# A two-layer hybrid diffusion step on one Trainium2 core: grouped-query products before the expansions, a two-operation silu, state products first, prompt scores in the value bank

## The chip, the cores and the metric

The kernel runs on one core of one Trainium2 chip. The metric is the device time of one execution in microseconds, as the median of several runs. A profile is one execution taken by the hardware profiler; its busy times are of the core's engines: PE (matrix products), DVE (vector), ACT (scalar functions and copies), POOL, and SP, whose queue issues DMAs.

## What is computed

One inference step over 128 prompt tokens and 512 noisy latent tokens, two layers of width 1024. Each layer is a modulated RMSNorm, one input projection, two branches side by side, one output projection and a gated residual. Layer 0 has multi-head latent attention (8 heads) and grouped-query attention (8 heads on 2 key heads); layer 1 has a bidirectional mLSTM and differential attention. The parts of the reference that the change touches:

```
u = h @ w_in
cq, ckv, kr, g_a, q_b, k_b, v_b, g_b = split_cols(u, EVEN_SPLITS)
q = (rmsnorm(cq, qn_g) @ w_uq)                      # expansion of the queries
q_b = rmsnorm(q_b.reshape(B, S, GQA_HEADS, GQA_HD), gq_g)
kv = (ckv_all @ w_ukv)                              # expansion of keys and values
o_a = attend(q_a, k_a, v_a) * jax.nn.silu(g_a)
o_b = attend(q_bg, kb_all, vb_all) * jax.nn.silu(g_b)
x + gate * (concatenate([o_a, o_b]) @ w_out)
# mLSTM: num = w_inter * (C q) + (Sm v)
```

## The kernel before

All products are made in float32 with operands split into a high and a low part, so that each is three matrix products (`mm3`, L81; lines L83, L84, L85): high by high, high by low, low by high. The five token groups of 128 (group 0 is the prompt) stand side by side.

The kernel is written as a program of tiles. A planner orders each engine's queue when the kernel is built, by the order in which the program states the instructions and by its own estimate of when each is ready; every engine then works through its queue in that order. Two tools bind it: `pe_order` (L162) fixes PE's order to the program's in the attention of layer 0, and `issue_after` puts the instructions of a block that run on one engine behind a given instruction of that engine.

The stages of layer 0, in order. `even_linear` (L342): the norm and modulation, then piece A of the input projection (compressed queries), piece B (compressed keys and values, grouped keys and values; `evB` L504), the query expansion in two halves (`evQ` L543), the value expansion (L553, its six results copied by DVE, L559), the key expansion (L561, copied by ACT), and piece C (grouped queries; `evC` L575: copy, sum of squares, norm, rotary embedding). Each result waits in one of five PSUM accumulators until ACT or DVE has copied it. `even_prep` (L768) builds the key tiles of the attention. `even_gates` (L591) makes the gate products and applies silu to each (`silu_from` L123).

`attention` (L699) runs over 16 heads. The scores of a head's four query blocks (L621) go to a ring of two score tiles (`s2`); DVE takes the row maximum (L628), ACT the exponential (L631), DVE the reciprocal (L634), POOL the scaling (L641). PE then transposes the scaled blocks (L648, `head_T`) into a ring of two (`t1`), ACT or DVE copies them (L653, L651), and PE multiplies them by the values (L659, `head_PV`) into the single tile `o`. While it transposes head h, the loop issues scores of heads h+1 and h+2. `prep` makes the split keys (`keys` L782, whose low part is a POOL subtraction, L789) and queries of head h+2. Four prompt quads (L663) go through four stages each between the heads; their scores (L672) take one of the two `s2` tiles. `side` (L860) adds the modulation products of layer 1, the gate products of layer 0 (L234), and loads and splits of the output projection's weights (L893); after head 15 it makes the row of residual gates (`ada_gate_row` L238, sum at L248). Then `out_proj` (L897) starts, with its accumulators in the PSUM banks of the attention.

In layer 1, `odd_linear` (L1035) makes the differential keys (`o_wK`), queries (`o_wQ`), values (`o_wV1`) and the mLSTM values (`o_wVM`); the mLSTM's scans over its gates (`mlstm_gates` L1221, on DVE and PE) are stated after the first of these. `mlstm_head` (L1447) makes, for each of five token groups, the product of scores and values (L1508, tile `pv`) and of state and query (tile `it`), and DVE adds the two (L1520); between them `adv` issues products of later pieces as filling, behind the instruction in `self.mark`.

Of the kernel before, what the change touches and what calls it, by code (L numbers as in the profile page):

```python
# [37 lines left out]
class K:  # L38
# [84 lines left out]
    def silu_from(self, out, src, shape, pool, other=None):  # L123

        nc = self.nc
        th = pool.tile(shape, F32, tag="th", name="th", bufs=2)
        nc.scalar.activation(out=th, in_=src, func=AF.Tanh, scale=0.5)
        nc.vector.tensor_scalar(out=th, in0=th, scalar1=0.5, scalar2=0.5, op0=ALU.mult, op1=ALU.add)
        nc.vector.tensor_tensor(out=out, in0=th, in1=src, op=ALU.mult)
        if other is not None:  # L130
            nc.vector.tensor_tensor(out=out, in0=out, in1=other, op=ALU.mult)
# [106 lines left out]
    def ada_gate_row(self, L, pool, tag, bufs):  # L238
# [9 lines left out]
        nc.vector.tensor_tensor(out=row, in0=ps[:, 0:256], in1=bias, op=ALU.add)  # L248
        for g in range(4):
            nc.sync.dma_start(self.gd[L][:, g * 256:g * 256 + 256], row[32 * g:32 * g + 2])  # L250
# [91 lines left out]
    def even_linear(self, E, EM, H, L, ps):  # L342
# [198 lines left out]

        for hf in range(2):
# [11 lines left out]
        for t in range(6):  # L554
# [4 lines left out]
            nc.vector.tensor_copy(Va[:, t, :], acc)  # L559
# [12 lines left out]

        self.qb = E.tile([128, 5, 512], F32, tag="qb", name="qb", bufs=1)

        def evC(t, acc):  # L575
            q = self.qb[:, t]
            nc.scalar.copy(q, acc)
            qv = q.rearrange("p (h w) -> p h w", h=8)
            r = self.rsqrt(self.sumsq(q, 8, 64), 8, 64)
            nc.vector.tensor_tensor(out=qv, in0=qv, in1=r[:, :, None].to_broadcast([128, 8, 64]), op=ALU.mult)  # L580
            nc.vector.tensor_tensor(out=qv, in0=qv, in1=self.rows[:, None, R_GQ:R_GQ + 64].to_broadcast([128, 8, 64]),
                                    op=ALU.mult)
            if t:
                self.rope(qv, qv, *ropeB(t), 8, 64, L)

        self.lin_tok([(A["e_wC"][i], 2) for i in range(4)], 512, Hh, Hl, range(5), evC, ps)

# [49 lines left out]
    def head_scores(self, T, ps, passes, i):  # L637
# [3 lines left out]
        self.nc.gpsimd.tensor_tensor(out=p, in0=p, in1=rs.to_broadcast([128, 640]), op=ALU.mult)  # L641
# [21 lines left out]
    def prompt_quad(self, T, ps, prep, V, cols, m):  # L663
# [4 lines left out]
        s = ps.tile([128, 2, 512], F32, tag="s2", name="sp", bufs=2)[:, 0]  # L668
# [1016 lines left out]
```

## Time and profile before

| | us |
|---|---|
| median of 3 runs | 885.71 |
| lowest and highest run | 885.25, 886.45 |
| the profiled execution, its own time | 888.68 |
| its span, first to last instruction | 886.9 |
| PE busy in the span | 839.8 |

A row of the waits names who waited, and the instruction that came last before it could go on. A row of a timeline merges neighbours of one kind: start, length, engine, line, operation, result and operands, shapes, count. Busy PE time contains the time in which PE works at half clock, so the granted clock is read beside it.

### The profile page before, as it was taken

How to read it: one execution, taken by the hardware profiler on the slowest of the kernel's cores; microseconds unless marked ns; L12 is line 12 of the kernel's file. 1: busy time of each engine (PE TensorE's matmuls, PEld its weight loads, DVE VectorE, ACT ScalarE, POOL GpSimd, SP SyncE). 2: the span in 40 equal slices, each digit the busy share in tenths (PEclk: the TensorE clock that was granted, in tenths of full speed). 3: DMA queues.
4: the chain of work that ended last, by engine and by line, in shares of the span. 5: the costliest groups of instructions: out<-in, count | busy, mean ns of one | idle time of the engine just before them, and what ended most of it. 6: DMA issues, size and time to landing. Idle time of an engine off the chain costs nothing.

```text
span 886.9 us, 14375 instructions
## 1 busy us (share of the span) xinstructions
PE 839.8 (95%) x5418; PEld 715.7 (81%) x5418; DVE 540.8 (61%) x1174; ACT 416.9 (47%) x920; POOL 258.5 (29%) x240
## 2 busy tenths in 40 slices
PE   5999999998999999899999999999999899999996
PEld 2778988997787876668888788889989688888886
DVE  3574932973665777525662864277674846667755
ACT  5354533323566777624442234266554656443423
POOL 0010201522666576713230000322220834230121
PEclk9999999999999999999999999999999999999999
DMA  9821322221122211454203222222123222143303
GB/s 343 349 67 36 109 70 71 79 87 51 48 96 96 96 49 55 137 207 137 116 25 131 84 77 84 72 72 73 48 96 132 71 79 62 59 173 113 125 1 119
DMA packets 29642, 88.52 MB, mean 100 GB/s; under 512 B 3753, under 2 KB 6881, under 8 KB 29573
## 3 DMA queue, kind: packets, MB, share of 16 engines
q1 hardware_dynamic: 25904, 83.64, 27.6%
q10 hardware_dynamic: 3668, 3.96, 1.4%
q8 instruction: 43, 0.70, 0.3%
q14 instruction: 27, 0.21, 0.1%
HBM read 80.90 MB, written 6.68 MB: 99 GB/s over the span
## 4 chain that ended last, share of the span: by engine, by line
PE 82%; DVE 5%; ACT 4%; POOL 3%; DMA 3%; issue 2%; SPq 0%; POOLq 0%; ACTq 0%; DVEq 0%
PE acc L83 13%; PE acc L85 13%; PE acc L84 13%; PE s L621 7%; PE acc L120 6%; PE acc L1108 6%; PE o L659 4%; PE t L648 3%; PE pv L1508 2%; PE o L1194 2%; PE ada L190 2%; POOL p L641 1%; DMA adaw<-in_eada_ss_dram 1%; PE acc L569 1%; PE accA L85 1%
## 5 line engine op out<-in xcount | busy, mean ns | idle before, releaser
L84 PE MATMUL acc<-wlo,Hh 128*128 128x512 f32 (+2 forms) x400 | 149.5, 374 | 0.0
L85 PE MATMUL acc<-whi,Hl 128*128 128x512 f32 (+2 forms) x400 | 149.1, 373 | 0.2 <-DVE Hl L1006 0.2
L83 PE MATMUL acc<-whi,Hh 128*128 128x512 f32 (+2 forms) x400 | 146.6, 377 | 2.4 <-ACT Hh L1004 1.4
L77 DVE TENSOR_TENSOR wlo<-raw,whi 128x1024 fp32r<-128x1024 f32 (+4 forms) x67 | 81.5, 1218 | 92.7 <-ACT whi L76 92.0
L76 ACT CAST whi<-raw 128x1024 fp32r<-128x1024 f32 (+4 forms) x71 | 71.5, 1007 | 126.8 <-PE acc L85 90.0
L628 DVE TENSOR_REDUCE nm<-s 128x1 f32<-128x640 f32 (+1 forms) x104 | 81.1, 781 | 53.2 <-PE s L621 52.2
L641 POOL TENSOR_TENSOR p<-p,rs 128x640 f32<-128x640 f32 x64 | 79.9, 1263 | 69.5 <-DVE rs L634 38.5
L631 ACT ACTIVATE p<-s,nm 128x640 f32<-128x640 f32 (+1 forms) x104 | 79.5, 765 | 41.5 <-DVE nm L628 38.6
L48 POOL TENSOR_TENSOR rs_r<-rs_h,mhalf 128x1 f32<-128x1 f32 (+4 forms) x39 | 40.1, 1032 | 195.8 <-DVE rs_h L47 195.6
L83 PEld LDWEIGHTS acc<-whi,Hh 128*128 128x128 f32 x400 | 75.8, 190 | 15.0 <-ACT Hh L1004 1.7
L85 PEld LDWEIGHTS acc<-whi,Hl 128*128 128x128 f32 x400 | 76.0, 190 | 13.6 <-DVE Hl L1006 0.4
L84 PEld LDWEIGHTS acc<-wlo,Hh 128*128 128x128 f32 x400 | 76.1, 190 | 12.3
L648 PE MATMUL t<-cst,p 128*128 128x128 f32 x320 | 49.1, 282 | 5.8 <-POOL p L641 3.5
L85 PE MATMUL acc<-whi,ol 128*128 128x512 f32 (+1 forms) x124 | 48.0, 387 | 0.0
L83 PE MATMUL acc<-whi,oh 128*128 128x512 f32 (+1 forms) x124 | 47.1, 388 | 0.9 <-DVE grow L248 0.9
L84 PE MATMUL acc<-wlo,oh 128*128 128x512 f32 (+1 forms) x124 | 47.9, 388 | 0.0
L648 PEld LDWEIGHTS t<-cst,p 128*128 128x128 f32 x320 | 38.4, 144 | 10.7 <-POOL p L641 5.0
L653 ACT COPY pT<-t 128x512 f32<-128x512 f32 x56 | 32.2, 587 | 25.2 <-PE t L648 24.9
L634 DVE RECIPROCAL rs<-sm 128x1 f32<-128x1 f32 x104 | 16.6, 159 | 28.6 <-ACT p L631 27.8
L621 PE MATMUL s<-Kb,q 128*128 128x320 f32 x128 | 27.7, 339 | 5.7 <-ACT pp L678 3.2
L1108 PE MATMUL acc<-Hh,whi 128*128 128x320 f32 x128 | 32.5, 323 | 0.5 <-ACT v L1085 0.5
L120 PE MATMUL acc<-Hh,whi 128*128 128x320 f32 x128 | 32.7, 309 | 0.0
(384 smaller groups left out, 1923.0 us busy)
## 6 DMA issues: line engine op xcount, KB each, us to landing
adaw<-in_eada_ss_dram SPq DMA_DIRECT2D x16, 512.0 KB, 10.2
raw<-in_oada_ss_dram SPq DMA_DIRECT2D x16, 512.0 KB, 3.5
raw<-in_e_wG_dram SPq DMA_DIRECT2D x8, 512.0 KB, 3.6
raw<-in_eada_g_dram SPq DMA_DIRECT2D x8, 512.0 KB, 3.5
raw<-in_e_wO_dram SPq DMA_DIRECT2D x8, 512.0 KB, 3.5
raw<-in_oada_g_dram SPq DMA_DIRECT2D x8, 512.0 KB
raw<-in_o_wO_dram SPq DMA_DIRECT2D x8, 512.0 KB, 7.1
xT<-in_xT_dram SPq DMA_DIRECT2D x8, 320.0 KB, 5.7
```

The source lines that it names most:

```text
L76: (cp or nc.scalar.copy)(hi[:, 0:m], raw[:, 0:m])
L77: (lo_on or nc.vector).tensor_tensor(out=lo[:, 0:m], in0=raw[:, 0:m], in1=hi[:, 0:m], op=ALU.subtract)
L83: mm(out, lhsT=lh, rhs=rh, start=first, stop=False)
L84: mm(out, lhsT=lh, rhs=rl, start=False, stop=False)
L85: self.mark = mm(out, lhsT=ll, rhs=rh, start=False, stop=last)
L120: mm(acc[j][:, 0:320], lhsT=a[:, k], rhs=b[:, k, j * 320:j * 320 + 320], start=f, stop=l)
L621: self.mark = self.nc.tensor.matmul(out[:, j, 0:w], lhsT=q[0:rows, qcols], rhs=k[0:rows, a:a + w], start=i == 0, stop=i == len(passes) - 1)
L628: nc.vector.tensor_reduce(out=nm, in_=s, axis=AX.XY, op=ALU.max, negate=True)
L631: nc.scalar.activation(out=p[:, 0:n].rearrange("p (a b) -> p a b", a=s.shape[1]), in_=s, func=AF.Exp, bias=nm, accum_out=sm)
L641: self.nc.gpsimd.tensor_tensor(out=p, in0=p, in1=rs.to_broadcast([128, 640]), op=ALU.mult)
L648: self.nc.tensor.transpose(tp[:, i * 128:i * 128 + 128], p[i][:, k * 128:k * 128 + 128], self.ident)
L1108: nc.tensor.matmul(acc[j][:, 0:320], lhsT=a[:, k], rhs=b[:, k, j * 320:j * 320 + 320], start=f, stop=l)
```

## The change

Eight edits, none of which changes the number of matrix products:

- Piece C of the input projection, with `evC`, moves from behind the key expansion to before the query expansion.
- The value expansion's results are copied by ACT, not DVE; so are the rotary key rows and the first two heads' high key parts in `even_prep`.
- silu is made by two operations, a tanh and one combined vector instruction, and is then twice as large; the gate row of layer 0 is halved once to make up for it.
- In the attention the scores (1, 1) are made before the loop; the preparation of keys is put behind the latest scaling on POOL; the passes of the latent scores take the low key part last.
- The prompt quads' scores go to the value tile `o`, and their stage is issued after the third transposition, in front of the next scores.
- The gate row of layer 0 is made before the last head's value products.
- The mLSTM gate scans move behind the third product of layer 1.
- In the mLSTM the state products are stated before the products of scores and values, and the mark for the filling is the last of the latter.

```diff
-        nc.vector.tensor_scalar(out=th, in0=th, scalar1=0.5, scalar2=0.5, op0=ALU.mult, op1=ALU.add)
-        nc.vector.tensor_tensor(out=out, in0=th, in1=src, op=ALU.mult)
...
+        self.nc.scalar.activation(out=th, in_=src, func=AF.Tanh, scale=0.5)
+        self.nc.vector.scalar_tensor_tensor(out=out, in0=th, scalar=1.0, in1=src, op0=ALU.add, op1=ALU.mult)
...
+        if L == "e":
+            nc.vector.tensor_scalar(out=row, in0=row, scalar1=0.5, scalar2=None, op0=ALU.mult)
...
         self.lin_tok([(A["e_wB"][i], 2) for i in range(4)], 512, Hh, Hl, (1, 2, 3, 4, 0), evB, ps)
...
+        self.lin_tok([(A["e_wC"][i], 2) for i in range(4)], 512, Hh, Hl, range(5), evC, ps)
...
-            nc.vector.tensor_copy(Va[:, t, :], acc)
+            nc.scalar.copy(Va[:, t, :], acc)
...
-        self.lin_tok([(A["e_wC"][i], 2) for i in range(4)], 512, Hh, Hl, range(5), evC, ps)
...
-                self.silu_from(self.og[:, m, j * 320:j * 320 + 320], acc[j], [128, 320], L)
+                self.silu2(self.og[:, m, j * 320:j * 320 + 320], acc[j], [128, 320], L)
...
-        self.nc.gpsimd.tensor_tensor(out=p, in0=p, in1=rs.to_broadcast([128, 640]), op=ALU.mult)
+        self.pm = self.nc.gpsimd.tensor_tensor(out=p, in0=p, in1=rs.to_broadcast([128, 640]), op=ALU.mult)
...
-        s = ps.tile([128, 2, 512], F32, tag="s2", name="sp", bufs=2)[:, 0]
+        s = ps.tile([128, 512], F32, tag="o", name="sp", bufs=1)
...
         scores(1, 0)
+        scores(1, 1)
...
             if h + 2 < nh:
-                prep[0](h + 2, P)
-            scores(h + 1, 1)
+                with self.tc.issue_after(self.pm.ins):
+                    prep[0](h + 2, P)
+            if h:
+                scores(h + 1, 1)
...
             pt.append(self.head_T(T, ps, p, 2, h))
+            done = stage(1)
             scores(h + 1, 3)
...
-            done = stage(0, 3)
+            done = done or stage(0, 3)
+            if h == nh - 1:
+                self.ada_gate_row("e", ps, "pr", 1)
             o = ps.tile([128, 512], F32, tag="o", name="o", bufs=1)
...
-            if not done:
-                stage(1, 2)
+            done = done or stage(2)
...
-                nc.vector.tensor_copy(Ka[s][i][RR[s]], krT[i][:, 0:640])
+                nc.scalar.copy(Ka[s][i][RR[s]], krT[i][:, 0:640])
...
-            nc.vector.tensor_copy(kh[NR[e]], src)
+            (nc.scalar.copy if h < 2 else nc.vector.tensor_copy)(kh[NR[e]], src)
...
-            P[h] = [(qh, kh, KR[e]), (qh, kl, KR[e]), (ql, kh, KR[e])]
+            P[h] = [(qh, kh, KR[e]), (ql, kh, KR[e]), (qh, kl, KR[e])]
...
-            if h == 15:
-                self.ada_gate_row("e", ps, "pr", 1)
...
-            if r is None:
+            if nm == "o_wV1":
                 r = self.mlstm_gates(M, Gp, ps)
...
+            if t:
                 it = ps.tile([128, 512], F32, tag="it", name="it", bufs=1)
                 ts = slice(t * 128, t * 128 + 128)
                 self.mm3(it[:, 0:258], qh[:, ts], ql[:, ts], ch, cl, True, True)
...
+                    self.mark = nc.tensor.matmul(acc[:, d * 129:d * 129 + 129],
```

## Rows read from the trace of the kernel before

**Rows 1.** The page, part 1: busy us and share of the span of each engine, with the number of instructions.
```profile
PE 839.8 (95%) x5418; PEld 715.7 (81%) x5418; DVE 540.8 (61%) x1174; ACT 416.9 (47%) x920; POOL 258.5 (29%) x240
```

**Rows 2.** Windows of stages: start:end and length in us, then for PE, PEld, DVE, ACT and POOL the busy us with the number of instructions, then PEclk, the granted TensorE clock (1.00 is 2.4 GHz, 0.50 is 1.2 GHz), DMA share, GB/s.
```profile
85.00:112.00 27.00, 26.53 (x144) 24.21 (x143) 24.89 (x96) 15.61 (x43) 7.24 (x10) 1.00 0.31 103
...
150.00:209.00 59.00, 59.00 (x399) 58.34 (x398) 43.20 (x85) 19.39 (x34) 19.54 (x13) 1.00 0.20 66
209.00:240.00 31.00, 25.42 (x180) 20.61 (x180) 17.01 (x37) 16.00 (x41) 16.65 (x14) 0.89 0.20 69
240.00:300.00 60.00, 59.46 (x531) 48.44 (x530) 39.54 (x88) 38.45 (x90) 37.12 (x29) 1.00 0.26 89
300.00:385.00 85.00, 76.01 (x667) 59.29 (x666) 55.77 (x117) 57.40 (x135) 56.11 (x43) 0.98 0.28 88
```

**Rows 3.** Waits of PE over the whole span, by the waiting line and its releaser: us in total, times, longest.
```profile
PE s L621 <- ACT pp L678: 4.2, 4, 2.7
...
PE t L648 <- POOL p L641: 3.5, 4, 2.1
...
PE s L621 <- DVE og L129: 1.5, 1, 1.5
PE pv L1508 <- DVE s L1497: 1.4, 1, 1.4
```

**Rows 4.** The timeline of PE in the linear stage, from the first product of the query expansion to the first of piece C (start us, us, engine, line, operation, shapes, count, and in brackets the idle time before it and what ended it).
```profile
87.38 0.34 PE L83 MATMUL acc<-whi,cqT 128*128 128x384 f32 x1
...
96.75 1.14 PE L83 MATMUL acc<-whi,cqT 128*128 128x384 f32 x5 [0.47 <-ACT whi L76]
...
113.76 0.50 PE L83 MATMUL acc<-whi,ckT 128*128 128x512 f32 x1 [0.46 <-ACT ckT L339]
...
123.82 0.39 PE L83 MATMUL acc<-whi,Hh 128*128 128x512 f32 x1
```

**Rows 5.** The timeline of ACT, then of DVE, around the evacuation of piece C (evC), same columns.
```profile
149.32 0.59 ACT L577 COPY qb<-acc 128x512 f32<-128x512 f32 x1 [3.16 <-PE acc L85]
...
155.15 0.69 DVE L581 TENSOR_TENSOR qb<-qb,rows 128x512 f32<-128x512 f32 x1
...
159.29 0.76 DVE L152 TENSOR_TENSOR ro<-qb,ropet 128x256 f32<-128x256 f32 x2
```

**Rows 6.** The timeline around the first scores, same columns.
```profile
209.44 0.65 DVE L128 TENSOR_SCALAR th<-th 128x320 f32<-128x320 f32 x2 [5.59 <-ACT th L127]
210.01 0.88 DVE L129 TENSOR_TENSOR og<-th,acc 128x320 f32<-128x320 f32 x2
...
210.55 0.85 PE L621 MATMUL s<-Ka,qh 96*128 96x320 f32 x4 [1.47 <-DVE og L129]
...
218.45 0.15 DVE L634 RECIPROCAL rs<-sm 128x1 f32<-128x1 f32 x1
...
218.67 1.54 POOL L789 TENSOR_TENSOR Ka<-kn,Ka 64x640 fp32r<-64x640 f32 x1 [2.26 <-DVE rs L634]
...
220.17 3.67 POOL L641 TENSOR_TENSOR p<-p,rs 128x640 f32<-128x640 f32 x3
...
221.47 0.33 PE L648 MATMUL t<-cst,p 128*128 128x128 f32 x1 [2.10 <-POOL p L641]
...
222.68 0.48 PE L648 MATMUL t<-cst,p 128*128 128x128 f32 x1 [0.88 <-POOL p L641]
```

**Rows 7.** Windows of one microsecond, columns as in the windows of stages.
```profile
213.00:214.00 1.00, 1.00 (x12) 0.41 (x10) 0.81 (x2) 0.69 (x3) 0.06 (x1) 0.50 0.00 0
...
223.00:224.00 1.00, 1.00 (x5) 1.00 (x5) 0.00 (x0) 0.58 (x1) 0.84 (x1) 0.50 0.00 0
...
350.00:351.00 1.00, 0.06 (x1) 0.00 (x0) 1.00 (x2) 1.00 (x3) 1.00 (x2) 1.00 0.00 0
...
363.00:364.00 1.00, 1.00 (x6) 1.00 (x5) 0.72 (x1) 0.20 (x1) 1.00 (x2) 0.50 0.29 45
```

**Rows 8.** The chain that ended last, two of its pieces in the latent heads: start us, us, what.
```profile
240.11 0.88 PE s L621 x6
240.99 0.88 PE t L648 x8
```

**Rows 9.** The timeline around the last prompt quad, same columns as the other timelines.
```profile
356.48 1.11 PE L672 MATMUL sp<-Kb,qp 128*128 128x128 f32 x8
...
357.63 0.69 DVE L674 TENSOR_REDUCE nm<-sp 128x4 f32<-128x512 f32 x1 [1.68 <-PE sp L672]
...
359.29 1.04 ACT L76 CAST whi<-raw 128x1024 fp32r<-128x1024 f32 x1 [0.62 <-DMA raw<-in_e_wO_dram]
...
360.24 0.36 ACT L678 ACTIVATE pp<-sp,nm 128x128 f32<-128x128 f32 x1
...
361.79 1.07 PE L621 MATMUL s<-Kb,q 128*128 128x320 f32 x4 [2.72 <-ACT pp L678]
```

**Rows 10.** The timeline at the end of the attention, same columns.
```profile
385.09 0.64 PE L245 MATMUL gsum<-gp,cst 128*32 128x256 f32 x8
385.21 0.87 DVE L747 TENSOR_TENSOR og<-o,og 64x256 f32<-64x256 f32 x2 [2.52 <-PE o L659]
...
386.11 0.42 DVE L248 TENSOR_TENSOR grow<-gsum,gbias 128x256 f32<-128x256 f32 x1
...
386.59 0.50 PE L83 MATMUL acc<-whi,oh 128*128 128x512 f32 x1 [0.86 <-DVE grow L248]
```

More of the change, by code (lines that the diff above doesn't have):

```diff
@@ L539, in even_linear, with evC @@
         self.lin_tok([(A["e_wB"][i], 2) for i in range(4)], 512, Hh, Hl, (1, 2, 3, 4, 0), evB, ps)
+        self.qb = E.tile([128, 5, 512], F32, tag="qb", name="qb", bufs=1)
+        def evC(t, acc):
+            q = self.qb[:, t]
+            nc.scalar.copy(q, acc)
+            qv = q.rearrange("p (h w) -> p h w", h=8)
+            r = self.rsqrt(self.sumsq(q, 8, 64), 8, 64)
+            nc.vector.tensor_tensor(out=qv, in0=qv, in1=r[:, :, None].to_broadcast([128, 8, 64]), op=ALU.mult)
+            nc.vector.tensor_tensor(out=qv, in0=qv, in1=self.rows[:, None, R_GQ:R_GQ + 64].to_broadcast([128, 8, 64]),
+                                    op=ALU.mult)
+            if t:
+                self.rope(qv, qv, *ropeB(t), 8, 64, L)
+        self.lin_tok([(A["e_wC"][i], 2) for i in range(4)], 512, Hh, Hl, range(5), evC, ps)
         for hf in range(2):
@@ L1502, in mlstm_head @@
         for t in range(5):
-            acc = ps.tile([128, 512], F32, tag="pv", name="pv", bufs=1)
-            for d in range(2):
-                js = [0] if t == 0 else (list(range(1, t + 1)) if d == 0 else list(range(t, 5)))
-                for i, j in enumerate(js):
-                    s, lo = sm[d][j]
-                    nc.tensor.matmul(acc[:, d * 129:d * 129 + 129], lhsT=s[:, t * 128 - lo:t * 128 - lo + 128],
-                                     rhs=v1[:, j, h], start=i == 0, stop=i == len(js) - 1)
-            av = acc[:, 0:258].rearrange("p (d v) -> p d v", d=2)
-            if t == 0:
-                nc.vector.tensor_copy(nd[:, t], av)
-            else:
+            if t:
                 it = ps.tile([128, 512], F32, tag="it", name="it", bufs=1)
@@ L1519, in mlstm_head @@
                                          scale=wi[:, t, col[d]:col[d] + 1])
+            acc = ps.tile([128, 512], F32, tag="pv", name="pv", bufs=1)
+            for d in range(2):
+                js = [0] if t == 0 else (list(range(1, t + 1)) if d == 0 else list(range(t, 5)))
+                for i, j in enumerate(js):
+                    s, lo = sm[d][j]
+                    self.mark = nc.tensor.matmul(acc[:, d * 129:d * 129 + 129],
+                                                 lhsT=s[:, t * 128 - lo:t * 128 - lo + 128],
+                                                 rhs=v1[:, j, h], start=i == 0, stop=i == len(js) - 1)
+            av = acc[:, 0:258].rearrange("p (d v) -> p d v", d=2)
+            if t == 0:
+                nc.vector.tensor_copy(nd[:, t], av)
+            else:
                 nc.vector.tensor_tensor(out=nd[:, t], in0=av, in1=nd[:, t], op=ALU.add)
```

19 lines of the change are left out of this document (2 added, 17 removed).

## The prediction, made before the change was run

> **What bounds the kernel now.** I read the page's engine shares first [rows 1]: PE is busy 839.8 of 886.9 us, every other engine at most 61%. The change leaves the number of matrix products as it is, so all it can win is PE's idle time, 47 us in the whole span, and time in which PE works at half clock. Then the windows by stage [rows 2], to see where that lies: the linear stage is as good as full (26.5 of 27 and 59.0 of 59 us), the latent heads in their steady part too (59.5 of 60), but the first 31 us of the attention hold 25.4 us of PE work at a mean clock of 0.89, and the 85 us with the grouped heads lack 9.0 us. Then PE's waits, for what ends the idle time [rows 3]; then the timelines of the places where these waits stand [rows 4 to 10]. A queue's order is set by a planner when the kernel is built, and I can't see the new order; where I count on it, I say so.
>
> **Part 1, piece C in front of the expansions; the value copies on ACT.** From the first query expansion to piece C it takes 123.82 - 87.38 = 36.4 us, with two waits in it, 0.47 us for a weight that ACT cast late behind the evacuation of piece B and 0.46 us for a compressed key of the same evacuation [rows 4]. With 28 us of piece C between them, both go: -0.9. What is late next is the evacuation of piece C itself. Its vector work is, per token group, a reduction and two products of about 0.69 us each and, for four of five groups, a rotary step of two such products and two half-size ones at 0.76 together [rows 5]: 5 x 2.1 + 4 x 2.1 = 19 us. It used to lie beside the gate products, where DVE was busy 43 of 59 us; now it lies beside the expansions, about 32 us of PE work with some 13 us of DVE work of their own (24.9 us of DVE in 27 us before, which held the tail of piece B too [rows 2]). That fills DVE, whose low weight parts PE needs. Nearest rows for a weight that is late: 0.47 us [rows 4]; for the worst, two whole vector products of 0.7 and a weight, some 2.3 us. I take +0.4. PE's accumulators are no rival: ACT copies the first at 149.32 in 0.59 us [rows 5] while PE still makes the last ones. Sum -0.5 (from -0.9 to +1.4).
>
> **Part 2, the first scores.** The scores wait 1.47 us for silu's last operations to leave the banks [rows 6]. The chain is tanh, 0.33 us for the tensor_scalar of the half that counts, then the product. One operation of the length of the old product (0.44 each) stands directly behind the tanh at 209.44, so the half is out at 209.9 and not 210.5: -0.6. The fifteen other silus lie under gate products with PE full; they win nothing.
>
> Next, the transpositions of head 0 wait 2.10 and 0.88 us for POOL [rows 6]. The scaling of block 2 could start at 218.6, when its reciprocal ends; POOL is in the 1.54 us key subtraction of head 2 from 218.67, so that scaling starts at 220.17 and the next ends at 222.65. The new edge puts the subtraction behind the scaling of (1, 1): scalings at 218.6 and 219.85, the second done at about 221.3, 1.35 us sooner. And the scores (1, 1), 0.88 us [rows 8], which followed the wait, now stand in it. Together -2.2. The subtraction now ends some 2.5 us later; cover is the 6 to 7 us until scores of head 2, whose pass with the low key comes last besides.
>
> Then the clock. After the wait of 1.47 us the granted clock stood at 0.50 at 213, after the wait of 3 us at 0.50 at 223, after one of 2.72 us at 0.50 at 363, and at 350, in an idle microsecond, it stayed at 1.00 [rows 7, 9]. The window from 209 to 240 has a mean of 0.89, that is 31 x 0.11 / 0.5 = 6.8 us at 1.2 GHz [rows 2], which cost half of it, 3.4 us. Both waits come down to under a microsecond, nearest to the one at 350, so I take all of it: -3.4, bounds 0 and -3.4. The Trainium skill, page "TensorE: Matmul & The Clock Gate", Part 1, says that the throttled state is the default, that activity lifts it, and that one and the same kernel shows different numbers of slow products in different runs. By that these 3.4 us are not owed to the waits alone, and the sum would be 3.4 less good; the trace, one execution, has each drop behind an idle stretch. Sum of part 2: -6.2 (from -2.0 to -6.8).
>
> **Part 3, prompt scores in the value tile.** Four times PE's scores waited for the exponentials of a quad, 4.2 us in all [rows 3], because these scores held one of two score tiles. That wait goes. In its place the value products of the head wait: their tile is now read by the quad's reduction (0.69 us) and four exponentials (360.24 to 361.75, 1.5 us) [rows 9], 2.2 us after the quad's scores. Between them PE has two rounds of scores and two transpositions, 0.88 + 0.88 + 0.88 us [rows 8] in latent heads, some 2.1 us with the four-product scores of grouped heads. So the cover just holds, if ACT is free. Queued behind the exponentials on ACT are the next scores' exponential and the copies of transpositions 3 and 4, which the value products need as well. I price it at what it replaces, 0 net, bounds -5.9 (the 4.2 us and the 1.7 us that the drop at 363 cost all go) and +11 (below). The 2.72 us at the last quad stood behind a weight cast that waited for its DMA until 359.29 [rows 9]; that cast is not moved, and what waits behind it next is the exponential of the scores.
>
> **Part 4, the gate row before the last value products.** PE's first product of the output projection stands 0.86 us for DVE's gate sum, which is queued behind the two gate products of head 15 [rows 10]; with the end of the sums at 385.73 that is PE idle or off the path from 385.2 to 386.59, 1.4 us. Made earlier, the sums cost about 0.5 us in a place where PE waits 0.2 to 0.3 us for a copy. Sum -1.1 (0 to -1.4). The halving is one short vector operation behind the sum, whose DMAs have the first 14 us of the projection as cover. SP gets the bias load a little earlier; nothing else queued there moves.
>
> **Part 5, layer 1.** The gate scans move past two products; PE had no idle microsecond there, and they get the third and fourth product, 28 us, as cover. 0 (up to +1). Stating the state product first lets PE make it inside the one wait of 1.4 us for masked scores [rows 3]; the timeline has it there already once, and the filling now stands behind products that can wait. -0.4 (from -1.4 to +1.5). The copies that go to ACT in `even_prep` lie under the gate products, where ACT is busy 19 of 59 us [rows 2]: 0.
>
> **Sum.** -0.5 - 6.2 + 0 - 1.1 + 0 - 0.4 = -8.2 us. It is made against the profiled execution, span 886.9 and own time 888.68, 3.0 above the median of 885.71; as a difference it goes on the median: 877.5.
>
> **The rivals.**
> - The clock falls at the start of the attention all the same, as behind any wait a little over a microsecond: -8.2 + 3.4, 880.9. For it: only one idle microsecond that left the clock alone stands against three that didn't. Against it: both waits shrink by 0.6 us or more.
> - The quads gain: the exponentials leave the scores' way for good and the clock doesn't fall at 363: -8.2 - 5 or so, 873. For it: the prompt stage now comes before the weight cast of `side` in the program. Against it: the cast still blocks ACT until its DMA lands.
> - The new order doesn't do what it says: the planner places other POOL work in front of the first scalings, or the expansions lose to the evacuation of piece C what the start gains. Then parts 2 and 1 shrink to -2 and +1.4, with part 4 -1.1: 884.0, no change.
> - Slower. The value tile becomes the bound: at each of four quads ACT has an exponential (0.8 + 0.2), a copy (0.6) and a cast (1.0) queued in front, so the value products wait 2.2 + 2.6 - 2.1 = 2.7 us, and each wait costs 1.7 us of half clock besides: 4 x 4.4 = 17.6, less the 5.9 that go, +11.7; with the rest -8.2, 889.2. It turns the sign by 1.8 us from a cost of 4 us per quad on, a wait of 2.3 us. For it: ACT is the busiest helper in the grouped heads, 57 of 85 us [rows 2]. Against it: in the latent heads it is at 38 of 60 us and two quads lie there.
>
> **How the numbers follow.** Forecast 877.5, chance 0.48; clock 880.9, 0.17; quads gain 873, 0.13; no effect 884.0, 0.12; slower 889.2, 0.10. A measurement of this kernel tells 0.2%, 1.8 us, from no change. The first three are faster by more: 0.78; same 0.12; slower 0.10. The range leaves out the slower case and half of the best one: 872.5 to 885.0. Its ends are the sum's own bounds in parts 2 and 3 as well.
>
> **What would show it.** In the profile after: the first scores about 0.8 us behind the last gate product; the window of 31 us from there with a mean clock of 0.95 or more; POOL's first subtraction behind six scalings; no wait of scores for the quads' exponentials, but waits of value products of under 0.5 us; the first projection product directly behind the last value product; the two waits of rows 4 gone and the expansions no longer than 35.5 us. Wrong would be the prediction above all if the value products wait 2 us at the quads, if ACT stands longer for the weight DMAs of the grouped heads in the new order, or if the expansions stretch beyond 37 us.

## The result and the profile after

The changed kernel takes 872.64 us (median of four runs, 872.32 to 873.69) against 886.08 for the kernel before beside it (885.25 to 888.35): ratio 0.9844, 95% interval 0.9825 to 0.9862. That is 13.4 us less, where the prediction had 8.2; taken as a difference from the kernel before, which is how the prediction carried its number over, its range allowed 13.2 at the most. Two later groups of runs gave 0.9866 (0.9845 to 0.9888) and 0.9859 (0.9841 to 0.9877); over the twelve runs the median is 873.2. The profiled execution has a span of 870.9 and an own time of 872.72, so it stands near its median, while that of before stood 3.0 above its own. Stages are therefore compared below by their own length, not by their place in the span.

Rows 1, page of the changed kernel, part 1: PE's busy time fell too, though the number of its products is the same (839.8 before). Most of that is products at the low clock: the profiled execution of before has four drops of the clock more than this one, and each makes PE 1.7 us longer.

```profile
PE 830.3 (95%) x5418; PEld 711.2 (82%) x5418; DVE 532.4 (61%) x1143; ACT 425.6 (49%) x936; POOL 249.8 (29%) x240
```

Windows of the changed kernel that answer to [rows 2]: the expansions, the gate products, the attention's first 30 us, the latent heads, the grouped heads (columns as there).

```profile
112.00:148.00 36.00, 36.00 (x192) 33.57 (x191) 29.66 (x74) 20.64 (x39) 10.22 (x5) 1.00 0.29 91
148.00:205.00 57.00, 57.00 (x392) 56.96 (x391) 16.13 (x25) 20.67 (x35) 6.75 (x8) 1.00 0.20 65
206.00:236.00 30.00, 27.16 (x222) 22.36 (x226) 21.17 (x44) 19.14 (x48) 20.20 (x17) 1.00 0.21 71
236.00:296.00 60.00, 59.56 (x534) 49.49 (x534) 41.05 (x89) 39.31 (x92) 35.80 (x29) 1.00 0.31 106
296.00:374.00 78.00, 69.03 (x635) 53.00 (x631) 51.92 (x108) 52.43 (x125) 53.27 (x41) 1.00 0.27 84
```

The third line is the one to compare: PE is busy 27.2 of 30 us at a clock of 1.00, where it had 25.4 of 31 at 0.89. DVE is idle 41 us in the gate stage, because piece C's evacuation now lies beside the expansions (first line: PE is full there and DVE busy 29.7 of 36 us).

Waits of PE in the changed kernel, whole span, to be read beside [rows 3]:

```profile
PE s L619 <- ACT p L629: 5.4, 8, 1.7
PE o L657 <- ACT pp L676: 3.1, 3, 1.3
PE t L646 <- POOL p L639: 2.2, 3, 1.5
...
PE pv L1516 <- DVE s L1498: 1.4, 1, 1.4
...
PE s L619 <- DVE og L127: 0.9, 1, 0.9
```

The scores' wait for the quads' exponentials (4.2) is gone. The value products wait 3.1 in its place, and the scores' wait for their own exponentials grew from 3.6 to 5.4. POOL's wait went from 3.5 to 2.2, silu's from 1.5 to 0.9; the 1.4 us of the masked products in layer 1 is untouched. The timeline of the start shows it in order (PE, then POOL):

```profile
206.35 0.56 PE L619 MATMUL s<-Ka,qh 96*128 96x320 f32 x2 [0.90 <-DVE og L127]
214.12 0.56 PE L619 MATMUL s<-Ka,qh 128*128 128x320 f32 x2 [0.67 <-ACT p L629]
216.00 0.76 PE L646 MATMUL t<-cst,p 128*128 128x128 f32 x5 [0.41 <-POOL p L639]
223.81 2.38 PE L657 MATMUL o<-pT,Va 128*64 128x256 f32 x20 [1.32 <-ACT pp L676]
...
216.28 2.46 POOL L639 TENSOR_TENSOR p<-p,rs 128x640 f32<-128x640 f32 x2 [0.33 <-DVE rs L632]
218.70 1.56 POOL L792 TENSOR_TENSOR Ka<-kn,Ka 64x640 fp32r<-64x640 f32 x1
```

The key subtraction stands behind the scalings, and the transpositions wait 0.41 where they waited 2.10 and 0.88 [rows 6]. The end of the attention, beside [rows 10]:

```profile
371.10 0.64 PE L241 MATMUL gsum<-gp,cst 128*32 128x256 f32 x8
371.67 2.38 PE L657 MATMUL o<-pT,Vb 128*64 128x256 f32 x20
373.98 0.50 PE L83 MATMUL acc<-whi,oh 128*128 128x512 f32 x1
```

The projection's first product follows the last value product with nothing between.

**Where the time came from, by stage.** Each length runs between two PE rows of the same kind in the two profiled executions:

| stage | before | after | difference | forecast |
|---|---|---|---|---|
| last product of piece A to first gate product | 95.1 | 93.4 | -1.7 | -0.5 |
| first gate product to first scores | 58.5 | 57.9 | -0.6 | -0.6 |
| first scores to last value product | 174.2 | 167.3 | -6.9 | -5.6 |
| last value product to the first transposition of the residual | 47.7 | 46.2 | -1.5 | -1.1 |
| last of these transpositions to the first of the differential heads | 119.5 | 118.4 | -1.1 | 0 |
| masked products of the mLSTM to the end of its transpositions | 147.1 | 145.3 | -1.8 | -0.4 |

The rest of the two spans' 16.0 us is the start-up, where piece A ended 1.9 earlier, and the products behind the last stage, 0.5 shorter. No part of the change touches the start-up: the profile of before has a drop of the clock at 21 us there, worth 1.7, and that of after has none. The attention, the only large term, came out near its forecast; of the small ones only silu's did. Which part makes each difference was left to the experiments.

### The profile page after: what moved, and what is told of

Read it like the earlier page. It is cut to its first block, busy times and chain, and to the rows that moved or that the text cites. A ratio compares the mean times of both kernels' runs of the same rounds, so it can differ in the third digit from the quotient of the medians.

```text
span 870.9 us, 14357 instructions
## 1 busy us (share of the span) xinstructions
PE 830.3 (95%) x5418; PEld 711.2 (82%) x5418; DVE 532.4 (61%) x1143; ACT 425.6 (49%) x936; POOL 249.8 (29%) x240
## 4 chain that ended last, share of the span: by engine, by line
PE 79%; DVE 7%; POOL 5%; ACT 3%; issue 3%; DMA 2%; SPq 0%; POOLq 0%; ACTq 0%; DVEq 0%
PE acc L83 13%; PE acc L85 13%; PE acc L84 13%; PE acc L120 6%; PE s L619 6%; PE acc L1109 6%; PE o L657 3%; PE t L646 3%; PE pv L1516 2%; PE o L1195 2%; PE ada L186 2%; POOL p L639 1%; PE acc L583 1%; DMA raw<-in_o_wO_dram 1%; PE accA L85 1%
## 5 line engine op out<-in xcount | busy, mean ns | idle before, releaser
L48 POOL TENSOR_TENSOR rs_r<-rs_h,mhalf 128x1 f32<-128x1 f32 (+4 forms) x39 | 36.9, 950 | 148.8 <-DVE rs_h L47 148.5
L646 PE MATMUL t<-cst,p 128*128 128x128 f32 x320 | 46.9, 276 | 3.1 <-POOL p L639 2.2
L619 PE MATMUL s<-Ka,qh 96*128 96x320 f32 (+1 forms) x128 | 31.6, 329 | 1.7 <-DVE og L127 0.9
L1109 PE MATMUL acc<-Hh,whi 128*128 128x320 f32 x128 | 32.5, 323 | 0.5 <-ACT v L1086 0.5
L1148 POOL TENSOR_TENSOR kdl<-ckd,kdh 128x128 fp32r<-128x128 f32 x8 | 3.6, 461 | 100.9 <-ACT kdh L1147 100.9
```

Of the source, the lines that this page charges most:

```text
L619: self.mark = self.nc.tensor.matmul(out[:, j, 0:w], lhsT=q[0:rows, qcols], rhs=k[0:rows, a:a + w], start=i == 0, stop=i == len(passes) - 1)
L646: self.nc.tensor.transpose(tp[:, i * 128:i * 128 + 128], p[i][:, k * 128:k * 128 + 128], self.ident)
L1109: nc.tensor.matmul(acc[j][:, 0:320], lhsT=a[:, k], rhs=b[:, k, j * 320:j * 320 + 320], start=f, stop=l)
```

## The experiments

The theory: each stage's surplus belongs to the part that edits it, so parts 1 and 5 were sized too small. The rivals: the surplus lies in the attention (quads, clock); or it is a difference between executions. Each experiment was timed in five rounds beside the kernel before.

**Single parts of the change, on the kernel before.** `a_linear` has this and the matching removal of piece C's old place:

```
+        self.lin_tok([(A["e_wC"][i], 2) for i in range(4)], 512, Hh, Hl, range(5), evC, ps)
         for hf in range(2):
             def evQ(t, acc, hf=hf):
...
-            nc.vector.tensor_copy(Va[:, t, :], acc)
+            nc.scalar.copy(Va[:, t, :], acc)
```

> The kernel before with part 1 alone: piece C in front of the expansions and the six value copies on ACT. By the prediction's term it is 0.5 us shorter (from 0.9 shorter to 1.4 longer). By the theory that each stage's gain in the two traces belongs to the part that edits that stage, it is 1.8 us shorter, since the time from the end of piece A to the first gate product went from 95.2 to 93.4 us. Told apart by the stage in the profile: 94.7 or 93.4 us.

Ratio 1.0001 (0.9986 to 1.0015). The stage did go to 93.4, but the gate products behind it took 60.1 us where they had taken 56.4. The timeline of PE, then of DVE, and two windows, all of a_linear:

```profile
158.22 0.66 PE L810 MATMUL qtp<-cst,qa 128*128 128x128 f32 x4 [1.89 <-DVE ql L340]
...
147.78 3.59 DVE L778 CAST Ka<-krt 32x640 fp32r<-32x640 f32 x4 [0.92 <-PE acc L585]
151.41 1.01 DVE L788 CAST Ka<-kn 64x640 fp32r<-64x640 f32 x2
152.45 2.48 DVE L77 TENSOR_TENSOR wlo<-raw,whi 128x1024 fp32r<-128x1024 f32 x1
154.96 1.86 DVE L779 CAST kp<-krt 32x256 fp32r<-32x256 f32 x2
...
157.47 0.69 DVE L340 TENSOR_TENSOR ql<-qtp,qh 128x512 fp32r<-128x512 f32 x1
```

```profile
158.00:160.00 2.00, 1.78 (x12) 1.78 (x13) 1.92 (x4) 0.59 (x1) 0.75 (x2) 0.88 0.01 2
160.00:162.00 2.00, 2.00 (x9) 2.00 (x8) 2.00 (x6) 0.00 (x0) 0.00 (x0) 0.50 0.22 39
```

The last expansion is now the key expansion, so `even_prep` may begin as soon as it ends, and DVE works 9.6 us without a gap, 7 of them on its key copies; the low part of head 0's queries stands behind them, PE waits 1.89 for it, and the clock then stands at 0.50. What part 1 wins is lost again to that wait. The drop of the clock behind it adds nothing to the total, because one of the two drops at the attention's start is missing in this execution; over its twelve runs the mean clock is 0.992, as in the kernel before. `ap_linear_copies` adds the copies' move to ACT (that of `kp` beside it, in the same form):

```
-                nc.vector.tensor_copy(Ka[s][i][RR[s]], krT[i][:, 0:640])
+                nc.scalar.copy(Ka[s][i][RR[s]], krT[i][:, 0:640])
...
-            nc.vector.tensor_copy(kh[NR[e]], src)
+            (nc.scalar.copy if h < 2 else nc.vector.tensor_copy)(kh[NR[e]], src)
```

> Part 1 and, with it, the preparing copies of layer 0's keys on ACT. Theory: the wait of 1.89 us for the low part of the queries in a_linear came from the key copies that stood on DVE in front of it (3.59 us of four copies and four more), so with the copies on ACT it is gone, the clock doesn't fall behind it, the gate products take 56.4 us again and the stage in front of them stays at 93.4: 1.8 us shorter in all. Rival: the wait comes from piece C's evacuation, whose last rotary steps lie late on DVE; then it stays, and the time is that of before. The prediction: 0.5 shorter.

Ratio 0.9980 (0.9966 to 0.9993), 1.8 us shorter; between the end of piece A and the first scores PE has no wait but that for silu. The rival, piece C's evacuation, falls. So the copies, which the prediction priced at 0, are the condition of part 1.

`b_start`: the early scores (1, 1), the edge on POOL, the order of the key passes and the same copies.

```
+        scores(1, 1)
         rest = None
...
             if h + 2 < nh:
-                prep[0](h + 2, P)
-            scores(h + 1, 1)
+                with self.tc.issue_after(self.pm.ins):
+                    prep[0](h + 2, P)
+            if h:
+                scores(h + 1, 1)
```

> The kernel before with the attention's start alone: scores (1, 1) early, the key subtraction behind the scalings, the low-key pass last, the preparing copies on ACT; silu stays in three operations, so the first wait of 1.47 us stays. By the prediction's terms POOL's part gives 2.2 us, and if the clock drop at 213 stays with that wait but the one at 223 goes, half of 3.4 more: 3.9 shorter. By the rival that the clock falls anyway: 2.2 shorter, with a granted clock of 0.5 near 213 and near 223. By the rival that the whole surplus of the attention (7.0 us in the two traces) lies here: 6 or more shorter.

Ratio 0.9946 (0.9926 to 0.9966), 4.8 us, next to the 3.9 of the prediction's terms. In its profile POOL's wait is 1.3 in place of 3.5, the drop near 223 is gone and the one behind silu's wait of 1.5 stands. Less its drops, the attention is 167.4 us against 169.1 before.

`f_silu`: silu in two operations and the halved gate.

```
-        nc.vector.tensor_scalar(out=th, in0=th, scalar1=0.5, scalar2=0.5, op0=ALU.mult, op1=ALU.add)
-        nc.vector.tensor_tensor(out=out, in0=th, in1=src, op=ALU.mult)
...
+        self.nc.vector.scalar_tensor_tensor(out=out, in0=th, scalar=1.0, in1=src, op0=ALU.add, op1=ALU.mult)
```

> The two-operation silu and the halving of the gate alone. The first scores' wait falls from 1.47 to 0.9 us: 0.6 shorter. By the prediction the clock drop near 212 goes too, 1.7 more; by the rival that a drop comes by chance behind some waits and not behind others, it may stand or not: between 0.6 and 2.3 shorter, and a drop behind POOL's wait near 222 as before.

Ratio 0.9984 (0.9968 to 1.0000), 1.4 us. The first wait is 0.9, as in after. The clock did not stay up all the same: behind POOL's waits of 3.0 us (2.3 and 0.7) it fell for twice as long as at any one place in before. A window of f_silu:

```profile
218.00:226.00 8.00, 5.99 (x27) 5.61 (x27) 1.88 (x4) 2.81 (x7) 3.64 (x4) 0.57 0.00 0
```

`c_quads`: the quads' tile and the step's place.

```
-        s = ps.tile([128, 2, 512], F32, tag="s2", name="sp", bufs=2)[:, 0]
+        s = ps.tile([128, 512], F32, tag="o", name="sp", bufs=1)
...
             pt.append(self.head_T(T, ps, p, 2, h))
+            done = stage(1)
             scores(h + 1, 3)
```

> The kernel before with part 3 alone: prompt scores in the value tile and their step in front of the last scores of the head. By the prediction 0 (it took the wait of the value products to be as long as the one that goes). By the rival that the quads gain: 4.2 us of waits of scores go, 3.1 us of waits of value products come (as in the trace of after), and the clock drop at 363, 1.7 us, goes: 2.8 to 5 us shorter. By the rival with the value tile as the bound: 11 us longer.

Ratio 1.0012 (0.9998 to 1.0027): no gain. Waits of PE in c_quads:

```profile
PE t L648 <- POOL p L641: 5.9, 5, 2.1
...
PE s L621 <- ACT p L631: 5.1, 8, 1.9
...
PE o L659 <- ACT pp L678: 2.1, 3, 1.3
```

The 4.2 us of [rows 3] are gone, 2.1 stand before the value products, 2.4 more before POOL's scalings (3.5 before) and 1.5 more before the scores' own exponentials (3.6 before).

`d_state`: the state product ahead of the masked ones, with the mark on the latter.

```
+            if t:
+                it = ps.tile([128, 512], F32, tag="it", name="it", bufs=1)
+                self.mm3(it[:, 0:258], qh[:, ts], ql[:, ts], ch, cl, True, True)
...
             acc = ps.tile([128, 512], F32, tag="pv", name="pv", bufs=1)
...
-                self.mm3(it[:, 0:258], qh[:, ts], ql[:, ts], ch, cl, True, True)
```

> The kernel before with the state product in front of the masked products alone. By the prediction 0.4 us shorter (1.4 shorter to 1.5 longer). By the theory that the stage's gain in the two traces is its own, 2.2 us shorter, the time from the first masked product to the first transposition of the mLSTM's result having gone from 122.7 to 120.5 us. By the rival that this difference is one of the two executions, under 0.5 us.

Ratio 0.9980 (0.9965 to 0.9996), 1.8 us; the stage of the mLSTM is 145.3 in place of 147.1, and the products from there to the end take 0.5 less, as two more of them now stand before its last transpositions: 2.3 in all. In a_linear, b_start and c_quads, which don't touch it, the stage is 147.1 to 147.2, so this is no difference between executions. Waits of PE in the mLSTM, first the kernel before:

```profile
PE st L83 <- DVE s L1497: 1.5, 2, 1.0
...
PE pv L1508 <- DVE nd L1520: 0.5, 1, 0.5
PE it L83 <- ACT nd L1518: 0.4, 1, 0.4
```

and d_state:

```profile
PE pv L1515 <- DVE s L1497: 1.4, 1, 1.4
...
PE st L83 <- DVE s L1497: 0.3, 1, 0.3
PE acc L83 <- DVE z L1417: 0.3, 1, 0.3
PE it L83 <- ACT nd L1508: 0.2, 1, 0.2
```

The wait of 1.4 us that the prediction meant to fill is still there. What went is the next head's first score products (1.5 to 0.3), and the 0.5 for a tile that DVE's addition held.

`ge_gates`: the gate row and the gate scans, in stages of their own.

```
+            if h == nh - 1:
+                self.ada_gate_row("e", ps, "pr", 1)
             o = ps.tile([128, 512], F32, tag="o", name="o", bufs=1)
...
-            if r is None:
+            if nm == "o_wV1":
                 r = self.mlstm_gates(M, Gp, ps)
```

> The kernel before with the gate row early and the gate scans of layer 1 in front of the last two products, nothing else. The two lie in stages of their own. Gate row: the time from the last value product to the first transposition of the residual 47.7 us before; by the prediction 46.6, by the trace of after 46.2. Gate scans: by the prediction 0; by the theory that the 1.1 us of that stage in the two traces are theirs, 107.7 in place of 108.8 from the last of those transpositions to the first differential scores; but a run of the state product alone shows 107.3 there as well, which speaks for a difference between executions. In all 1.1 to 2.6 shorter.

Ratio 0.9970 (0.9956 to 0.9985), 2.7 us. The first stage is 46.2 us, as in after. The gate sums themselves now stand in the attention: from the start of the last four transpositions to that of the value products it takes 0.59 us before and 1.15 here, so 0.56 of the 1.5 is paid there. The second took 116.9 us against 119.5. Part of that is the clock: before, it fell there for 3.4 us at 461, which costs 1.7, and in d_state and f_silu, where it did not fall, the stage is 118.0. So the scans' move is worth 118.0 - 116.9 = 1.1. Its mechanism is visible in PE's order. The timeline before:

```profile
506.17 0.39 PE L83 MATMUL acc<-whi,Hh 128*128 128x512 f32 x1
506.49 0.43 PE L1277 MATMUL gtp<-cst,Q 36*128 36x36 f32 x4
506.85 0.50 PE L84 MATMUL acc<-wlo,Hh 128*128 128x512 f32 x1
507.19 0.39 PE L85 MATMUL acc<-whi,Hl 128*128 128x512 f32 x1
```

and ge_gates:

```profile
530.17 0.28 PE L85 MATMUL acc<-whi,Hl 128*128 128x256 f32 x1
530.38 1.06 PE L1277 MATMUL gtp<-cst,Q 36*128 36x36 f32 x14
531.37 0.50 PE L83 MATMUL acc<-whi,Hh 128*128 128x512 f32 x1
531.70 0.39 PE L84 MATMUL acc<-wlo,Hh 128*128 128x512 f32 x1
```

Two products of 512 columns take 0.45 from start to start; with four small transpositions of 36 rows between them the same stretch is 1.02, 0.57 more. Before, fifteen such transpositions stood in five places, with 1, 4, 5, 1 and 4, and cost 0.38, 0.57, 0.63, 0.40 and 0.58: some 0.32 for each place and 0.06 for each transposition. Moved, fourteen stand in one place and cost 1.2, by that rule 0.32 + 14 x 0.063 = 1.20. Three places fewer are the 1.0. Transpositions of 128 rows don't show such a cost: in the output projection of before, one between two such products adds 0.12 us and four add 0.45, that is 0.11 each and next to nothing for the place. So the cost goes with the 36 rows. The Trainium skill, page "TensorEngine Tiling (Array Packing)", section "Tiling Modes", says that a change of tiling mode drains the engine, while another tile of the same mode does not; the trace agrees in so far as about 0.3 us go with each change from 128 rows to 36 and back, but no run shows the mode itself.

**The change with one part undone.** `u_no_start` takes back what b_start adds, the copies included; `u_no_quads` what c_quads adds. Their diffs are those above, reversed.

> The changed kernel with the order at the attention's start undone: scores (1, 1) late again, no edge on POOL's subtraction, the key passes and the preparing copies as before; silu, piece C, quads and the rest as changed. By the prediction's terms POOL's 2.2 us come back and with them a drop of the clock behind that wait (1.7 to 3.4): 3.9 to 5.6 longer than the changed kernel. By what a_linear showed, the key copies on DVE also make the gate products wait again, 1.9 and 1.7 of clock: up to 9 longer. If the silu alone kept the clock up, 2.2 to 4.1 longer.

879.46 against 874.38 for the changed kernel in the same group: 5.1 longer (ratios to before 0.9935, 0.9917 to 0.9954, and 0.9866). Waits of PE from 150 to 380 us in it:

```profile
PE t L646 <- POOL p L639: 6.1, 5, 2.3
...
PE qtp L810 <- DVE ql L338: 1.9, 1, 1.9
```

Both effects are there: POOL's waits are back, with a clock drop at 222, and so is a_linear's 1.9 in the gate products, with one at 160.

> The changed kernel with part 3 undone: prompt scores in a score tile again, their step at the end of the head. By the theory that the quads gain only where POOL's order is mended (c_quads had 2.4 us more of POOL's waits): the scores' waits for the quads, 4.2 to 4.9 us, come back, the 3.1 us of value products' waits and about 1.5 us of the scores' waits for exponentials go, and a clock drop near the last quad comes back, 1.7: 1 to 4 us longer than the changed kernel, attention 168.5 to 171 us from the first scores to the last value product against 167.3. By the prediction's 0 and by c_quads alone: as long as the changed kernel, or 1 shorter.

874.62, ratio 0.9876 (0.9855 to 0.9896), against 0.9844 for the changed kernel in another group. Attention 168.5. Since that left the quads between 0 and 3 us, both ran again side by side:

> The changed kernel again, as the partner of the next one: 872.5 to 874.5 us.

> The changed kernel with part 3 undone, beside the changed kernel in one group. By the prediction's 0 the two agree within 0.5 us; by the attention of the two profiles, 168.5 against 167.3 with no clock drop in either, the kernel with part 3 undone is 1.2 longer; by the two earlier groups it is 2 to 2.8 longer.

873.19 against 875.04, ratios 0.9859 (0.9841 to 0.9877) and 0.9881 (0.9864 to 0.9897). The intervals overlap; the profiles are sharper. Without the quads the attention took 168.5 with no clock drop, then 170.2 with one of 1.7, that is 168.5 again; with them 167.3, 167.6 and, in a third execution, 167.7 less its drops. So the quads are worth about 1.0 us, and only beside the other edits: alone they were worth nothing. That POOL's order makes the difference fits the 2.4 us more of POOL's waits in c_quads, but was not tested by itself, and the 1.0 is not in PE's waits: PE is idle 11.9 us in the attention of after and 11.7 in that of u_no_quads, two executions without a drop there.

**The clock.** The changed kernel once more:

> The changed kernel once more, for the comparison with the others of this group and for a second look at its clock: about 1.45% below the kernel before, 872.6 us. By the theory that the clock stays up because no wait at the start is long, no microsecond below 0.9 between the first scores and the last value product here either; by the rival of chance, one or two drops of about 3.4 us, each costing 1.7.

Ratio 0.9866 (0.9845 to 0.9888). Two drops in the grouped heads, none in the attention's first 30 us. Value products at the last quad, first in the changed kernel's first profile, then in this one:

```profile
344.36 2.38 PE L657 MATMUL o<-pT,Vb 128*64 128x256 f32 x20 [1.29 <-ACT pp L676]
```

```profile
344.51 4.07 PE L657 MATMUL o<-pT,Vb 128*64 128x256 f32 x20 [1.29 <-ACT pp L676]
```

The same instructions behind the same wait of 1.29 us, at full clock and at half of it. What a drop costs is always the same: the sum of one minus the clock over one-microsecond windows gives 1.7, or 3.4 for a long one. Counted from the first scores to the last value product (loss in us, at the start and in the last heads):

| start as before | at the start | last heads | start as changed | at the start | last heads |
|---|---|---|---|---|---|
| before | 3.4 | 1.7 | after | 0 | 0 |
| a_linear | 1.7 | 1.7 | after_again | 0 | 3.4 |
| c_quads | 3.4 | 0 | after_third | 0 | 0 |
| d_state | 3.4 | 0 | u_no_quads | 0 | 0 |
| ap_linear_copies | 3.4 | 0 | u_no_quads_again | 0 | 1.7 |
| ge_gates | 3.4 | 1.7 | | | |

At the start each of six executions with the old order lost 1.7 or 3.4, none of five with the new one lost anything. The silu wait of 1.5 us alone does not decide it: a_linear has it and kept the clock behind it. Of the four variants below, which share the new start, three lost nothing there either; v_quad_early lost 1.7 at 225 us, behind a new wait of 1.36 us for DVE. In the last heads drops come and go on both sides. (b_start, with silu's wait left, lost 1.7 at the start, f_silu, with POOL's left, 3.4.)

**Can the new waits be taken away?** Three variants of the changed kernel. `v_quad_early` puts `done = stage(1)` behind the second transposition in place of the third.

> The changed kernel with the quads' scores one step earlier, in front of the third scores of the next head rather than of the fourth. Theory: the value products' waits for the exponentials, 3.1 us in after, come from these starting too late, and one round of scores and one of transpositions more, 0.88 + 0.27, covers most of it: 1.5 to 2.5 us shorter. Rival: ACT is the limit at a quad, so that the exponentials moved ahead only delay the scores' own exponential: waits of scores for it, 5.4 us in after, grow by as much, same time within 0.7.

Ratio 0.9922 (0.9899 to 0.9944) against 0.9866: 4.5 us longer than the changed kernel beside it, which neither theory had. Waits of PE from 150 to 380 us:

```profile
PE s L619 <- ACT p L629: 5.8, 8, 2.1
PE t L646 <- DVE pT L649: 3.0, 3, 1.1
PE s L619 <- DVE ql L338: 2.0, 2, 1.4
PE t L646 <- POOL p L639: 1.4, 3, 0.6
```

The value products no longer wait; DVE takes their place. The quad's maximum stands early in its queue, and the copy of a transposition and the low part of the queries stand behind it: 5.0 us of waits for DVE that the changed kernel does not have. `v_one_exp`:

```
...
-        for j in range(4):
-            nc.scalar.activation(out=p[:, j], in_=s[:, 128 * j:128 * j + 128], func=AF.Exp, bias=nm[:, j:j + 1],
-                                 accum_out=sm[:, j:j + 1])
+        nc.scalar.activation(out=p.rearrange("p a b -> p (a b)"), in_=s, func=AF.Exp, bias=nm)
+        nc.vector.tensor_reduce(out=sm, in_=p, axis=AX.X, op=ALU.add)
...
```

> The changed kernel with one exponential of 512 columns in a quad in place of four of 128, with one maximum for the four heads and the sums by a reduction on DVE (the softmax is the same but for rounding). In after the four take 0.37 and 0.21 us each, 2.3 in all; one of 512 by the length of one of 640 is about 0.8. If ACT is the limit at the quads, the value products' waits (3.1 us) go and the scores' waits for exponentials (5.4) shrink: 3 to 5 us shorter. If DVE's late maximum is the limit (the first quad's exponentials stood 2.77 us for it), the new reduction of 0.7 on DVE delays the following maxima: within 0.7 of the changed kernel.

Ratio 0.9864 (0.9847 to 0.9882), the same as the changed kernel. The value products' wait fell from 3.1 to 1.0, POOL's rose from 2.2 to 3.6: the wait has gone over to POOL, where the quad's scaling and the heads' scalings share one queue. `v_load_early` moves four weight loads one head forward; `v_load_one_exp` has both edits.

```
-            if h >= 12:
-                self.op_load("e_wO", 0, h - 12, lo_on=self.nc.gpsimd)
+            if 11 <= h < 15:
+                self.op_load("e_wO", 0, h - 11, lo_on=self.nc.gpsimd)
```

> The changed kernel with the four output weight loads of heads 12 to 15 one head earlier. In after the cast of such a weight stood on ACT until 350.85, 1.30 us for its DMA, with the scores' exponential behind it, and PE's scores waited 1.75 for that. If the load in time lets ACT run through, 1.3 to 1.8 us shorter (more if a drop of the clock behind that wait goes with it, as one stood in the second profile of after). Rival: the buffer of the load comes free no earlier, or the next load stands for its DMA instead: same within 0.5.

> The two edits of v_one_exp and v_load_early together in the changed kernel. If both waits are ACT's, 2 to 3.5 us shorter than the changed kernel; if the waits only go over to POOL, as in v_one_exp (its waits rose from 2.2 to 3.6 us), no better than v_load_early.

Ratios 0.9875 (0.9861 to 0.9889) and 0.9874 (0.9857 to 0.9891), against 0.9859: no gain in either. The rival held: ACT in v_load_early stood 1.63 us for the load, longer than the 1.30 before it was moved, and PE's scores 2.08 behind it.

```profile
354.50 1.04 ACT L76 CAST whi<-raw 128x1024 fp32r<-128x1024 f32 x1 [1.63 <-DMA raw<-in_e_wO_dram]
```

No variant beats the changed kernel by more than its measurement is uncertain.

## Why the prediction was too small

The direction and the largest term were right, and the forecast's sum failed in small terms that were sized on the low side. The runs show it without the profiles: with each run's loss to the clock taken off (its span times one minus its mean clock), the changed kernel is 9.0 us below the kernel before in the group of after_again and 9.2 in that of after_third. The forecast without its clock term was 4.8. The clock brought 2.4 and 3.6 us more, where the forecast had 3.4.

- **Part 1, forecast -0.5, measured -1.7: mis-sized.** The two waits went, as said. But they were read from PE's idle time (0.47 and 0.46 [rows 4]), and a matmul's end in the page is modelled. The weight loads show the same two stalls at 0.7 each and a third of 0.2, in all 1.6 (rows below). And the +0.4 for weights that DVE would deliver late did not come: from 112 to 148 us PE was busy 36.00 of 36 with DVE at 29.7. The end that the range kept open, +1.4, was real in another place: a_linear lost 1.9 and 1.7 to DVE's key copies. The prediction looked at these copies under the gate products of before and gave them 0; in the new order they come earlier, and their move is worth the 1.9 us of that wait (ratio 1.0001 without it, 0.9980 with it). The 1.7 is no net gain, as the clock fell elsewhere instead.
- **Part 2, forecast -6.2: right in its steps.** Silu's wait fell by 0.57. POOL's order, forecast 2.2, was worth 1.7 alone (attention of b_start less its two drops, 170.8 - 3.4 = 167.4, against 174.2 - 5.1 = 169.1 before); behind the sooner silu the scores then wait 0.67 us for the exponentials, in the timeline of after. The clock's 3.4 is what before lost, 3.1 on the mean of the six executions in the table, and the first rival, that it falls anyway, is refuted at the start: these executions kept it. f_silu shows that one of the two waits alone does not keep it up. By the page that the prediction named ("TensorE: Matmul & The Clock Gate", Part 1, of the Trainium skill) the number of slow products at a kernel's start differs between runs of one kernel; in the last heads something like it shows, 0, 3.4 and 0 us in three executions of the same program; at the attention's start it does not.
- **Part 3, forecast 0, measured about -1.0, beside the other edits only.** The trade of waits was seen rightly: 4.2 us go, 3.1 come before the value products (1.32, 0.53 and 1.29 us; under 0.5 each was named as the sign) and 1.8 before the scores' own exponentials. Of the signs listed it is the one that came out wrong; the expansions, now 32.7 us from their first product to the first gate product, the clock, POOL's order and the projection's first product came as named. The slower rival needed 2.3 us at each quad; the longest was 1.32.
- **Part 4, forecast -1.1, measured -0.9: right.** Its stage got 1.5 shorter, and the sums cost 0.56 in their new place, inside the attention.
- **Part 5, forecast -0.4, measured -3.4: the step that failed.** The gate scans were priced at 0 because PE had no idle microsecond there; they cost PE time without idling it, 0.3 us for each place where transpositions of 36 rows break into the products, and three such places went: 1.1. The state product was said to fill the 1.4 us before the masked products, for 0.4. That wait stayed; what shrank were the 1.5 us before the next head's scores, a row that the prediction had not used, and the 0.5 behind DVE's addition, together by 1.7; from the stage's first product to the kernel's end it is 2.3.
- **The range.** The prediction says that its ends are the sum's own bounds in parts 2 and 3 as well. They are not: with part 3 at its best bound the sum gives 871.6, below the lower end, and with part 2 at its worst 881.7, well inside.

The rows that part 1 should have used, waits of PEld from 57 to 153 us in the kernel before:

```profile
PEld acc L83 <- ACT whi L76: 0.7, 1, 0.7
PEld acc L83 <- ACT ckT L339: 0.7, 1, 0.7
PEld acc L84 <- DVE wlo L77: 0.2, 1, 0.2
```

With these sizes: 1.7 + 0.57 + 1.8 (attention less its drops: mean 169.3 in before, a_linear, ap_linear_copies, d_state and ge_gates, 167.5 in the three profiles of after; the gate sums' 0.56 is in it) + 3.1 + 1.5 + 1.1 + 2.3 = 12.1, against 13.4 in the first group, 11.4 and 12.7 in the later ones. What is left is spread between executions, of which the start-up is a part: in kernels that share its code piece A ended from 56.5 to 57.2 us where the clock fell near 21 us, and from 54.2 to 55.7 where it did not.

What stays open: why the clock falls behind 1.29 us of waiting in one execution and not in the next, how the quads win their 1.0, and how much of it is owed to the edge on POOL rather than to the early scores, which were not tried apart.

## What to carry to other kernels

Price a stall from the weight loads' waits as well as from the matmuls', and take the longer. A move that lets a stage begin sooner also lets everything that stage has queued begin sooner: list it, by engine, before pricing it at nothing. Where waits of several engines stand at one place, a part that removes one of them may measure nothing alone (the quads, piece C) and something together with the part that removes the next.

## What the runs showed of the hardware

Transpositions of 36 rows between products of 128 rows cost PE about 0.3 us for each place where they break in and 0.06 us each, where those of 128 rows cost 0.11 each and next to nothing for the place. No wait of PE names it; only start-to-start times and five idle stretches of 0.35 us of the weight loads, put down to "issue", show it. A drop of the clock lost 1.7 us wherever it was seen, or twice that, and one program's runs spread by such steps: the changed kernel's runs from 871.11 to 874.94 us have mean clocks from 0.999 down to 0.994.
